# Two-part float32r products: one 512-column matmul over both parts of the activations, the halves added behind

## The chip, the cores and the metric

One core of one Trainium2 chip runs the kernel. The metric is device time in microseconds (us) of one execution. TensorE (PE) multiplies, with weight loads (PEld) beside its products; VectorE (DVE), ScalarE (ACT) and GpSimd (POOL) do the elementwise work; SyncE (SP) issues most of the DMAs.

## What is computed

Two transformer blocks of different make, one after the other, on 256 tokens of 1024 features, all in float32. The first has two layers: sparse attention with an output projection, a feed-forward, dilated attention with an output projection, a feed-forward. The second has one layer: a feed-forward, a mixer of three branches (indexed attention, a state-space layer, attention to a memory) with an output projection, a feed-forward. There are thus four feed-forwards of 2816 hidden features:

```python
def swiglu(h, w_up, w_down):
    a, b = jnp.split(h @ w_up, 2, axis=-1)
    return (jax.nn.silu(a) * b) @ w_down

x = x + swiglu(rmsnorm(x, norm_ffn[layer]), ffn_w_up[layer], ffn_w_down[layer])   # first block
x = x + 0.5 * swiglu_ffn(rms_norm(x, ffn1_norm[l]), ffn1_w_in[l], ffn1_w_out[l])  # second block
```

and three output projections of 1024x1024 (`... @ w_out`) that are added to x.

## The kernel before

Activations are held transposed: a tile is 128 features (partitions) by 256 tokens (S = 256). x is eight such tiles.

Precision: a float32 operand is split into two parts of type float32r, a high part (a rounding copy, on ACT) and a low part (the difference, on DVE). A product of two split operands is the sum of three products: high weight with high activations (line 228), high weight with low activations (229), low weight with high activations (230). `mm3` issues them for every weight block of 128x128 into one PSUM bank; the weight block is the stationary operand, the 256 columns of an activation part are the moving one. So each weight block costs three matmuls of 256 columns, and each of them loads its stationary operand. The page writes a matmul as out<-moving,stationary: `ov<-hh,wh` is high part of hidden block by high weight.

Weights come from HBM in loads of 128 x 8 x 256 float32 (1 MB, line 178, on SP's queue; tile `raw`, four buffers). `split` (lines 187 and 188) makes `wh` on ACT and `wl` on DVE, 1024 columns at a time (8 blocks, one projection's worth of the up phase), with four buffers of each.

`proj` takes the next PSUM bank (in the wide stages a rotation over seven of the eight banks, `take`) and runs `mm3` over all blocks of the inner dimension.

`ffn`, up phase: for each of 22 hidden blocks two projections (gate and up) over 8 blocks of x. DVE multiplies each with the row factors R of the norm while it reads PSUM (lines 393 and 395), ACT applies Silu (396), DVE multiplies (397), ACT and DVE split the hidden block into `hh` and `hl` (400, 401), which are two tiles. Down phase, `out_proj`: for each of 8 output tiles one projection over 22 hidden blocks, then one DVE multiply-add into x (411). The three output projections of attention and mixer go through `out_proj` too, with 8 blocks each. `gsplit` and `split_act` make the two parts of x and of attention outputs, as two tiles.

The order of instructions on each engine is made by a planner which lists them by priority and a modelled timeline; a stage's loads and splits so run ahead of it, and side work (the preparation of the state-space layer, `s5_prepare`, and the norm of the memory, `mem_norm`) lies where the planner found room: between 540 and 660 us, in the up phase of the second feed-forward. Buffers and semaphores follow from that order; every engine works its own list in order.

## Time and profile before

| | |
|---|---|
| median of 3 runs | 1362.96 us (1362.46 to 1367.53) |
| the profiled execution | 1365.27 us, its span 1363.5 us |
| TensorE busy | 1336.2 us (98%), 10944 products |
| weight loads busy | 1266.6 us (93%) |
| DVE busy | 1003.5 us (74%) |
| ACT busy | 746.7 us (55%) |
| POOL busy | 185.2 us (14%) |
| granted clock of TensorE | 0.994 |
| DMA | 232.77 MB, mean 171 GB/s |

The page gives busy time by engine, the span in 40 slices, the chain that ended last, and the costliest groups of instructions. A row of a group reads: line, engine, operation, tiles as out<-in, shape and type, count, then busy time in us, mean time of one in ns, idle time of the engine ahead of them with what ended it. Matmuls are pipelined, and each is printed with a length that overlaps the next: the cost of one in a stream is the distance of the starts.

### The profile page before, as it was taken

The numbers are of one execution on the slowest core, as the hardware profiler recorded it, in microseconds if no ns is written. First come the engines' busy times: TensorE is split into PE (matmuls) and PEld (weight loads), VectorE is DVE, ScalarE is ACT, GpSimd is POOL, SyncE is SP. The second block draws the span as 40 slices with busy tenths as digits, with TensorE's granted clock in tenths as the row PEclk, the third lists the DMA queues.
The fourth block names the chain that finished last, engine by engine and source line by source line (L and its number), as shares of the span: only waits on it lengthen the run. The fifth ranks groups of instructions, "written<-read, shape, count | busy, mean of one in ns | idle before, by whom it ended". The sixth has DMA issues, their size and how long they took to land.

```text
span 1363.5 us, 27489 instructions
## 1 busy us (share of the span) xinstructions
PE 1336.2 (98%) x10944; PEld 1266.6 (93%) x10944; DVE 1003.5 (74%) x2119; ACT 746.7 (55%) x1414; POOL 185.2 (14%) x225
## 2 busy tenths in 40 slices
PE   8999999999999999999999999999999999999997
PEld 7886999999998887999999999999987879999997
DVE  6899677766797663998955877755598897777643
ACT  4677555545668785754544555544433565544442
POOL 4200100001210000322100310001121044000011
PEclk9999999999999999999999999999999999999999
DMA  9741365545766350466856465556744254555451
GB/s 287 245 157 63 109 200 187 186 140 195 238 212 181 104 140 9 153 199 201 259 178 208 156 212 191 179 171 203 222 132 147 78 170 155 190 187 188 152 194 50
DMA packets 227120, 232.77 MB, mean 171 GB/s; under 512 B 5944, under 2 KB 221184, under 8 KB 226992
## 3 DMA queue, kind: packets, MB, share of 16 engines
q1 hardware_dynamic: 223392, 226.14, 52.3%
q10 hardware_dynamic: 3600, 4.88, 1.0%
q8 instruction: 86, 1.41, 0.4%
q14 instruction: 42, 0.34, 0.1%
HBM read 226.69 MB, written 4.30 MB: 169 GB/s over the span
## 4 chain that ended last, share of the span: by engine, by line
PE 85%; DVE 8%; DMA 2%; issue 2%; ACT 1%; POOL 1%; SPq 0%; POOLq 0%; DVEq 0%; ACTq 0%
PE mm L228 10%; PE mm L230 10%; PE mm L229 10%; PE tr L230 6%; PE tr L228 6%; PE tr L229 6%; PE sc L230 6%; PE sc L228 6%; PE sc L229 5%; PE ov L473 3%; PE ov L228 3%; PE ov L230 3%; PE ov L229 3%; DVE wl L188 3%; PE sc L777 2%
## 5 line engine op out<-in xcount | busy, mean ns | idle before, releaser
L187 ACT ACTIVATE wh<-raw 128x1024 fp32r<-128x1024 f32 (+2 forms) x405 | 417.8, 1036 | 449.9 <-PE mm L229 158.9
L188 DVE TENSOR_TENSOR wl<-raw,wh 128x1024 fp32r<-128x1024 f32 (+2 forms) x405 | 491.9, 1217 | 167.4 <-ACT wh L187 162.9
L228 PE MATMUL mm<-xh,wh 128*128 128x256 f32 x952 | 270.9, 285 | 2.4 <-ACT wh L187 2.4
L229 PE MATMUL mm<-xl,wh 128*128 128x256 f32 x952 | 270.9, 285 | 0.0
L230 PE MATMUL mm<-xh,wl 128*128 128x256 f32 x952 | 269.9, 284 | 0.5 <-DVE wl L188 0.5
L228 PEld LDWEIGHTS mm<-xh,wh 128*128 128x128 f32 x952 | 181.2, 190 | 9.7 <-issue 5.3
L230 PEld LDWEIGHTS mm<-xh,wl 128*128 128x128 f32 x952 | 180.7, 190 | 5.5 <-issue 4.0
L229 PEld LDWEIGHTS mm<-xl,wh 128*128 128x128 f32 x952 | 181.2, 190 | 3.1 <-issue 2.8
L293 POOL TENSOR_TENSOR sqacc<-sqacc,sq 128x256 f32<-128x256 f32 x60 | 61.8, 1033 | 602.7 <-ACT sq L292 326.1
L228 PE MATMUL sc<-xh,wh 128*128 128x256 f32 x464 | 129.7, 279 | 1.8 <-ACT wh L187 1.8
L230 PE MATMUL sc<-xh,wl 128*128 128x256 f32 x464 | 129.5, 279 | 0.2 <-DVE wl L188 0.2
L229 PE MATMUL sc<-xl,wh 128*128 128x256 f32 x464 | 129.5, 279 | 0.0
L230 PE MATMUL tr<-xh,wl 128*128 128x256 f32 x440 | 123.1, 280 | 0.4 <-DVE wl L188 0.4
L229 PE MATMUL tr<-xl,wh 128*128 128x256 f32 x440 | 122.8, 279 | 0.0
L228 PE MATMUL tr<-xh,wh 128*128 128x256 f32 x440 | 122.8, 279 | 0.0
L228 PEld LDWEIGHTS sc<-xh,wh 128*128 128x128 f32 x464 | 87.6, 189 | 2.0 <-ACT wh L187 2.0
L229 PEld LDWEIGHTS sc<-xl,wh 128*128 128x128 f32 x464 | 87.6, 189 | 0.0
L230 PEld LDWEIGHTS sc<-xh,wl 128*128 128x128 f32 x464 | 87.2, 188 | 0.4 <-DVE wl L188 0.4
L230 PEld LDWEIGHTS tr<-xh,wl 128*128 128x128 f32 x440 | 82.7, 188 | 0.6 <-DVE wl L188 0.6
L229 PEld LDWEIGHTS tr<-xl,wh 128*128 128x128 f32 x440 | 83.1, 189 | 0.0
L228 PEld LDWEIGHTS tr<-xh,wh 128*128 128x128 f32 x440 | 83.1, 189 | 0.0
L228 PE MATMUL ov<-xh,wh 128*128 128x256 f32 x224 | 62.7, 280 | 0.0
(481 smaller groups left out, 3404.9 us busy)
## 6 DMA issues: line engine op xcount, KB each, us to landing
raw<-in_ffn_w_up_dram SPq DMA_DIRECT2D x44, 1024.0 KB, 5.3
raw<-in_ffn_w_in_dram SPq DMA_DIRECT2D x44, 1024.0 KB, 5.3
raw<-in_w_in_dram SPq DMA_DIRECT2D x17, 1024.0 KB, 5.4
raw<-in_ffn_w_down_dram SPq DMA_DIRECT2D x16, 1024.0 KB, 5.2
raw<-in_ffn_w_out_dram SPq DMA_DIRECT2D x16, 1024.0 KB, 5.2
raw<-in_b_w_q_dram SPq DMA_DIRECT2D x12, 1024.0 KB, 5.2
raw<-in_a_w_in_dram SPq DMA_DIRECT2D x8, 1024.0 KB, 8.7
bt<-u_scratch SPq DMA_DIRECT2D x28, 256.0 KB, 4.5
```

Of the source, the lines that this page charges most:

```text
L187: nc.scalar.activation(hv, v, AF.Copy)
L188: nc.vector.tensor_tensor(lv, v, hv.bitcast(F32), ALU.subtract)
L228: nc.tensor.matmul(ps, sh, mh, start=(i == 0), stop=False)
L229: nc.tensor.matmul(ps, sh, ml, start=False, stop=False)
L230: nc.tensor.matmul(ps, sl, mh, start=False, stop=(i == n - 1))
L293: nc.gpsimd.tensor_tensor(acc[:, 0], acc[:, 0], s, ALU.add)
L473: nc.tensor.matmul(O[64 * i:64 * i + 64, q0:q1], V[kb], pt[:, c0:c0 + q1 - q0], start=(start and kb == 0), stop=(stop and kb == 1), skip_g ...
L777: nc.tensor.matmul(ps, Q[d, h][:, qb * P:qb * P + P], K[d][g], start=(i == 0), stop=(i == 1))
```

## The change

`mm2` takes the place of `mm3` in the feed-forwards and in `out_proj`. The two parts of an activation block now lie side by side in one tile of 512 columns (`parts`): the high weight meets both in one product of 512 columns that fills a whole PSUM bank, and the low weight meets the high part in one product of 256 columns that adds to the bank's first half. The result is the sum of the bank's halves. In the up phase `joined` makes it: ACT copies the second half to SBUF (`fc`), DVE adds the first half to it, POOL multiplies with R, which DVE did before. In `out_proj` DVE adds each half to x in a multiply-add of its own. The buffers of `fa` and `fb` go from two to three, `fc` has three. Other projections keep `mm3`, on the halves of the joint tiles.

```diff
--- before.py
+++ after.py
@@ -224,10 +224,18 @@
 
         nc = self.nc
         n = len(pairs)
-        for i, ((sh, sl), (mh, ml)) in enumerate(pairs):
+        for i, ((sh, sl), (mh, ml, *_)) in enumerate(pairs):
             nc.tensor.matmul(ps, sh, mh, start=(i == 0), stop=False)
             nc.tensor.matmul(ps, sh, ml, start=False, stop=False)
             nc.tensor.matmul(ps, sl, mh, start=False, stop=(i == n - 1))
+
+    def mm2(self, ps, pairs):
+
+        nc = self.nc
+        n = len(pairs)
+        for i, ((sh, sl), (mh, _, mhl)) in enumerate(pairs):
+            nc.tensor.matmul(ps, sh, mhl, start=(i == 0), stop=(i == n - 1), skip_group_check=True)
+            nc.tensor.matmul(ps[:, :S], sl, mh, start=False, stop=(i == n - 1), skip_group_check=True)
 
     def bank(self, tag):
         return getattr(self, tag).tile([P, 512], F32, tag=tag, name=self.n(tag))
@@ -246,23 +254,33 @@
         self.mm3(o, list(zip(unit, X)))
         return o
 
+    def proj2(self, unit, X):
+
+        o = self.take()
+        self.mm2(o, list(zip(unit, X)))
+        return o[:, :S], o[:, S:]
+
     def proj_tok(self, wide, X, tb, cols):
         o = self.take()[:, :cols]
         sl = slice(tb * P, tb * P + P)
-        self.mm3(o, [((xh[:, sl], xl[:, sl]), w) for (xh, xl), w in zip(X, wide)])
+        self.mm3(o, [((xh[:, sl], xl[:, sl]), w) for (xh, xl, _), w in zip(X, wide)])
         return o
+
+    def parts(self, pool, tag, name, **kw):
+
+        hl = pool.tile([P, 2 * S], F32R, tag=tag, name=self.n(name), **kw)
+        return hl[:, :S], hl[:, S:], hl
 
     def split_act(self, src, name, k, pool=None, flip=False):
 
         nc = self.nc
         src = flipped(src) if flip else blocks(src)
         pool, pre = (pool, name) if pool else (self.xs_pool, "x")
-        h = pool.tile([P, S], F32R, tag=f"{pre}h{k}", name=self.n(name + "h"))
-        l = pool.tile([P, S], F32R, tag=f"{pre}l{k}", name=self.n(name + "l"))
+        h, l, hl = self.parts(pool, f"{pre}{k}", name)
         h3, l3 = blocks(h), blocks(l)
         nc.scalar.activation(h3, src, AF.Copy)
         nc.vector.tensor_tensor(l3, src, h3.bitcast(F32), ALU.subtract)
-        return h, l
+        return h, l, hl
 
 
     def gain(self, name, k):
@@ -271,11 +289,10 @@
     def gsplit(self, x, g, k):
 
         nc = self.nc
-        h = self.xs_pool.tile([P, S], F32R, tag=f"xh{k}", name=self.n("xh"))
-        l = self.xs_pool.tile([P, S], F32R, tag=f"xl{k}", name=self.n("xl"))
+        h, l, hl = self.parts(self.xs_pool, f"x{k}", "x")
         nc.scalar.activation(h, x, AF.Copy, scale=g)
         nc.vector.scalar_tensor_tensor(l, x, g, h.bitcast(F32), ALU.mult, ALU.subtract)
-        return h, l
+        return h, l, hl
 
     def sq_begin(self):
         return self.tmp.tile([P, 2, S], F32, tag="sqacc", name=self.n("sqacc"), bufs=1)
@@ -387,28 +404,33 @@
                 ub = self.units(w_up, D, FF + mp * 256)
                 for c in range(2):
                     k = 2 * mp + c
-                    pa = self.proj(next(ua), X)
-                    pb = self.proj(next(ub), X)
-                    a = hp.tile([P, S], F32, tag="fa", name=self.n("fa"), bufs=2)
-                    nc.vector.tensor_tensor(a, pa, R, ALU.mult)
-                    b = hp.tile([P, S], F32, tag="fb", name=self.n("fb"), bufs=2)
-                    nc.vector.tensor_tensor(b, pb, R, ALU.mult)
+                    a, b = (self.joined(hp, next(u), X, R, t) for u, t in ((ua, "fa"), (ub, "fb")))
                     nc.scalar.activation(a, a, AF.Silu)
                     nc.vector.tensor_tensor(b, a, b, ALU.mult)
-                    h = hp.tile([P, S], F32R, name=self.n("hh"), tag=f"hh{k}")
-                    l = hp.tile([P, S], F32R, name=self.n("hl"), tag=f"hl{k}")
+                    h, l, hl = self.parts(hp, f"h{k}", "hh")
                     nc.scalar.activation(h, b, AF.Copy)
                     nc.vector.tensor_tensor(l, b, h.bitcast(F32), ALU.subtract)
-                    H.append((h, l))
+                    H.append((h, l, hl))
             self.out_proj(xs, w_down, FF, H, factor)
+
+    def joined(self, pool, unit, X, R, tag):
+
+        nc = self.nc
+        p, q = self.proj2(unit, X)
+        t = pool.tile([P, S], F32, tag="fc", name=self.n("fc"), bufs=3)
+        nc.scalar.activation(t, q, AF.Copy)
+        a = pool.tile([P, S], F32, tag=tag, name=self.n(tag), bufs=3)
+        nc.vector.tensor_tensor(a, p, t, ALU.add)
+        nc.gpsimd.tensor_tensor(a, a, R, ALU.mult)
+        return a
 
     def out_proj(self, xs, w, K, X, factor):
         nc = self.nc
         for mp in range(4):
             for c, u in enumerate(self.units(w, K, mp * 256)):
-                ps = self.proj(u, X)
                 m = 2 * mp + c
-                nc.vector.scalar_tensor_tensor(xs[m], ps, float(factor), xs[m], ALU.mult, ALU.add)
+                for ps in self.proj2(u, X):
+                    nc.vector.scalar_tensor_tensor(xs[m], ps, float(factor), xs[m], ALU.mult, ALU.add)
 
 
     def bias_rows(self):
```

## Rows read from the trace of the kernel before

**Rows 1.** The page: its head and the first line of section 1.

```profile
span 1363.5 us, 27489 instructions
PE 1336.2 (98%) x10944; PEld 1266.6 (93%) x10944; DVE 1003.5 (74%) x2119; ACT 746.7 (55%) x1414; POOL 185.2 (14%) x225
```

**Rows 2.** Table of stretches: start:end, length, busy us (count) by engine, clock, DMA.

```profile
171.00:350.00 179.00, 179.00 (x1522) 179.00 (x1522) 124.27 (x176) 91.85 (x131) 6.03 (x6) 1.00 0.58 186
560.00:680.00 120.00, 118.92 (x1037) 118.12 (x1036) 114.01 (x312) 68.28 (x108) 29.65 (x44) 1.00 0.65 208
685.00:745.00 60.00, 60.00 (x514) 60.00 (x513) 30.31 (x34) 25.74 (x31) 4.36 (x3) 1.00 0.60 196
797.00:880.00 83.00, 83.00 (x735) 83.00 (x734) 62.29 (x96) 43.78 (x64) 0.00 (x0) 1.00 0.60 192
888.00:945.00 57.00, 57.00 (x484) 57.00 (x483) 34.14 (x39) 26.88 (x37) 5.83 (x6) 1.00 0.59 188
1173.00:1288.00 115.00, 115.00 (x979) 115.00 (x978) 83.90 (x127) 58.87 (x84) 0.00 (x0) 1.00 0.56 182
1290.00:1349.00 59.00, 59.00 (x494) 59.00 (x493) 28.04 (x31) 23.43 (x29) 7.79 (x6) 1.00 0.40 130
```

**Rows 3.** Longest wait of TensorE from 560 to 680: us in total, times, longest.

```profile
PE tr L230 <- DVE wl L188: 0.4, 1, 0.4
```

**Rows 4.** Timeline of TensorE, second feed-forward up: start, length, instruction.

```profile
620.04 0.28 PE L228 MATMUL sc<-xh,wh 128*128 128x256 f32 x1
...
629.89 0.28 PE L228 MATMUL mm<-xh,wh 128*128 128x256 f32 x1
```

**Rows 5.** Timeline of TensorE: products of 512 columns in the first attention.

```profile
85.15 0.40 PE L642 MATMUL sc<-KH,q 128*128 128x512 f32 x1
85.39 0.39 PE L642 MATMUL sc<-KL,q 128*128 128x512 f32 x1
85.62 0.28 PE L230 MATMUL mm<-xh,wl 128*128 128x256 f32 x1
...
89.39 0.39 PE L642 MATMUL sc<-KH,q 128*128 128x512 f32 x1
89.61 0.39 PE L642 MATMUL sc<-KL,q 128*128 128x512 f32 x1
89.84 0.28 PE L229 MATMUL mm<-xl,wh 128*128 128x256 f32 x1
```

**Rows 6.** Groups by shape: the split from 171 to 265, the others over the span.

```profile
L188 DVE TENSOR_TENSOR wl<-raw,wh 128x1024 fp32r<-128x1024 f32 x34 | 41.7, 1226 | 10.5 <-ACT wh L187 9.4
L395 DVE TENSOR_TENSOR fb<-sc,R 128x256 f32<-128x256 f32 x26 | 10.9, 421 | 10.1 <-PE sc L230 10.1
L411 DVE SCALAR_TENSOR_TENSOR x<-tr,x 128x256 f32<-128x256 f32 x17 | 7.2, 421 | 13.4 <-PE tr L230 13.3
L810 ACT ACTIVATE Rd<-tr 128x256 f32<-128x256 f32 x8 | 3.0, 376 | 3.8 <-PE tr L808 3.7
```

**Rows 7.** Groups by shape over the span: POOL, and DVE beside it.

```profile
L1017 POOL TENSOR_TENSOR vr<-vr,t 128x256 f32<-128x256 f32 x8 | 5.9, 741 | 40.9 <-DVE t L1014 40.9
L490 POOL TENSOR_TENSOR KL<-kt,KH 64x256 fp32r<-64x256 f32 x20 | 20.1, 1005 | 22.4 <-ACT KH L487 21.5
L488 DVE TENSOR_TENSOR KL<-kt,KH 64x256 fp32r<-64x256 f32 x20 | 16.9, 845 | 0.3
L502 DVE TENSOR_TENSOR q<-qt,q 64x256 fp32r<-64x256 f32 x64 | 26.9, 420 | 2.0
```

**Rows 8.** Group of DVE from 560 to 680: the weight split.

```profile
L188 DVE TENSOR_TENSOR wl<-raw,wh 128x1024 fp32r<-128x1024 f32 x43 | 54.4, 1266 | 0.6 <-ACT wh L187 0.6
```

**Rows 9.** Timeline at the end of the last feed-forward.

```profile
1354.13 0.42 DVE L411 SCALAR_TENSOR_TENSOR x<-tr,x 128x256 f32<-128x256 f32 x1 [7.71 <-PE tr L230]
```

**Rows 10.** Timeline of TensorE where the first feed-forward ends.

```profile
350.28 0.28 PE L230 MATMUL tr<-hh,wl 128*128 128x256 f32 x1
350.40 0.28 PE L228 MATMUL mm<-xh,wh 128*128 128x256 f32 x1
```

## The prediction

> **What bounds the kernel now.** I read the page's busy shares first, then a table of stretches cut by stage, then the waits, then single products in the timeline. The busy shares name TensorE: 1336.2 of 1363.5 us [rows 1]. A share of busy time is an average, so the question is what each stage that the change touches waits for. Seven stretches lie inside the four feed-forwards [rows 2]: 171 to 350 is the whole first one, then come up and down of the second, the third and the fourth. In six of them TensorE is busy in every microsecond at a granted clock of 1.00 (2.4 GHz), DVE for 47 to 75% and ACT for 40 to 53%. DMA moves 130 to 196 GB/s with its engines busy for 0.40 to 0.60. These stages are worth what their products cost, one after the other. The seventh stretch, the up phase of the second feed-forward (560 to 680), differs: DVE is busy for 114.0 of 120 us there, its weight splits wait 0.6 us in all for their input [rows 8], and the longest wait of TensorE is for such a split [rows 3]. There DVE stands right behind TensorE.
>
> The price of a product is start to start, not the printed duration (products overlap). By stretch, busy time over products, less two that lap over the edges [rows 2]: first feed-forward 179/1520 = 0.1178 us; down phases of the other three 0.1172, 0.1183 and 0.1199; up of the third 0.1132; up of the fourth 0.1177. Up of the second, without its waits: 87 products from 620.04 to 629.89, 0.1132 [rows 4]. So 256 columns cost 0.113 to 0.120 where 256 cycles of 2.4 GHz are 0.1067: each product carries 0.0065 to 0.0133 on top, and the up phases at 0.1132 and at 0.1177 run the same code.
>
> **The change, part by part.** Products. Per weight block there were three of 256 columns; now there are one of 512 and one of 256. Blocks: a feed-forward has 44 x 8 going up and 8 x 22 coming down, 528, times four, 2112; the three output projections of attention and mixer have 64 each, 192; together 2304. TensorE spends on them now: first feed-forward 1584 x 0.1178 = 186.6; second 1056 x 0.1132 + 528 x 0.1172 = 181.4; third 119.5 + 62.5 = 182.0; fourth 124.3 + 63.3 = 187.6; the 576 products of the output projections at about 0.115 (an estimate between the two levels) 66.2. Sum 803.8 us.
>
> What does a product of 512 columns cost? The kernel has a few of the same operand type, in the scores of the first attention: start to start 0.22, 0.23, 0.24, 0.23 [rows 5], a mean of 0.23 with the last figure rounded. Those stand singly among other work. From the long streams: the common 256-column step of 0.1178 less 0.1067 is 0.0111 on top per product; with the same on top, 512 columns are 0.2133 + 0.0111 = 0.2244, the lower end of those rows. I take 0.2244, because an unbroken stream is what the feed-forwards are, and 0.1175 for the other product: 0.3419 per block, 2304 x 0.3419 = 787.7, a gain of 16.1 us. It is all of one kind: one of three amounts on top is dropped. Best end: 0.2133 + 0.0065 for the wide one and 0.1132 for the narrow one, 0.333, gain 36.6. Worst end: 0.24 and 0.1199, 0.360, loss 25; the 0.24 came once, so 0.23 + 0.1199 = 0.350, a loss of 2.5, is the end that I carry. The two stretches at 0.1132 gain nothing at my price (0.3396 now); the gain comes from the first and the fourth feed-forward and the down phases.
>
> The Trainium skill, "TensorE: Matmul & The Clock Gate", section "Back-to-back issue gap", speaks against the change: it gives a warm product its columns over 2.4 GHz plus 2.5 ns, and by that dropping a product would save 2304 x 0.0025 = 5.8 us. The trace doesn't agree with 2.5 ns here, since the least step of the streams has 6.5 ns on top.
>
> Halves, up phase. For each of 176 products (44 in each feed-forward) DVE's multiplication by R, 0.42 [rows 6], becomes an addition of the same size and operands (PSUM and SBUF): nothing. ACT gets a copy of 128x256 out of PSUM, 0.376 by a like copy [rows 6]: 44 x 0.376 = 16.5 us per up phase of some 120 us, on an engine that is half idle [rows 2]; covered. POOL gets the multiplication by R, 0.74 undisturbed [rows 7]: 44 x 0.74 = 32.6 us per up phase, on an engine that is idle in the first, third and fourth. In the chain to the hidden block, copy, POOL and three hand-overs add 1.3 us or more; the last hidden block is wanted only behind the first 21 blocks of the down product (21 x 0.342 = 7.2 us), so I cost it at nothing; without that cover it is some 2 us for each feed-forward. PSUM banks rotate over seven products of 2.7 us; one more reader does not fill them.
>
> What POOL does to DVE is the dearest unknown. Where both subtract the same tile in two halves, DVE's 64x256 takes 0.845 in place of 0.420, and POOL 1.005 [rows 7]: 0.425 per POOL instruction when DVE follows at once. The weight split, with two inputs from SBUF too, takes 1.226 in the quiet up phase and 1.266 in the second, where POOL works for 29.7 us [rows 2, 6, 8]. So a POOL instruction costs DVE between nothing and its own 0.74; I take 0.25, since a good third of DVE's work (the additions, and its idle time) takes nothing from POOL. In three up phases that is 11 us on an engine with 30 us to spare: covered by the splits made ahead. In the second, 44 x 0.25 = 11 us meets 6 us of idle time: TensorE waits 5 us more.
>
> The Trainium skill, "SBUF — State Buffer", section "Who interferes with whom", has this as a rule: a DVE instruction with two inputs from SBUF contends with a POOL instruction that reads SBUF, and whoever comes second waits for the whole of the other. The trace agrees for DVE's 0.845. By the rule's full wait, 0.74 each, the second up phase would lose 32.6 - 6 = 27 us; that is the third case below.
>
> Halves, down phase. Each of 56 output tiles gets a second multiply-add of 0.42 [rows 6]: 3.4 us per stage, beside an idle DVE. Between stages the first projection of the next stage follows without a gap (350.28 to 350.40 [rows 10]); I put 1 us for the six joints (0 to 2.5). At the very end it is bare: the last multiply-add begins when TensorE is done [rows 9], so +0.4.
>
> One tile for both parts: the first product waits for high and low part together, where it waited for the high one. That falls into the same 1 us. Loads, splits and queues of DMA stay as they are; 2 MB per 10.9 us in place of 11.3 asks 4% more of DMA engines that have a third of their time free.
>
> Sum: 16.1 - 5 - 1 - 0.4 = 9.7 us. The profiled execution took 1365.27 us (span 1363.5, 1.8 around it), 0.2% over the median of 1362.96. From it: 1355.6; set against the median: **1353 us**.
>
> **The rivals.** (1) The wide product has the price of the mean row, 0.23: 0.3475 per block, 800.6, a gain of 3.2, which the 6.4 us of other terms eat: 1366 us. For it: the rows themselves. Against it: in the streams the step is constant for tens of microseconds. (2) POOL holds DVE for its whole 0.74 in the second up phase: 1353 + 22 = 1375 us, slower. It decides from the point where the price reaches 0.62 per POOL instruction (then 27 - 6 = 21 us of waits use up what is left of the gain and the half per cent). For it: DVE has 6 us left in that stretch. Against it: 0.425 is the highest that the rows show. (3) The streams settle in the cheap step, 0.333 per block: 1353 - 20 = 1333 us. For it: two up phases run at 0.1132 now, with the same code. (4) Instructions are ordered by a planner, and new durations give a new order in every stage: some 4 us either way, 1357 us if it goes against the kernel. That the products are not saved is not among the rivals; 2304 fewer are in the code.
>
> **How the numbers follow.** Forecast 0.48, (1) 0.21, (2) 0.14, (3) 0.08, (4) 0.09. A measurement tells about 0.5% (6.8 us) from no change, so faster means below 1356.1 and slower above 1369.8. Faster: (3) and nine tenths of the forecast, with a little of (4), 0.53; slower: (2) and a little of (1), 0.16; the rest, 0.31, is no change. The range runs from 1337 (half of (3) left out) to 1372 (most of (2) left out).
>
> **What would show it.** TensorE's products 2304 fewer; in the stretch of the first feed-forward a pair of steps of 0.224 and 0.118 where three of 0.118 stood; the first feed-forward shorter by some 6 us and the fourth by 7, the up phases of the second and third not shorter. A longer second up phase with DVE at its limit, and waits of TensorE for the weight split, would be case (2); the weight split's mean there tells the price. A wide step of 0.23 is case (1). The forecast is wrong if the narrow product behind a wide one costs other than 0.113 to 0.120, or if products wait for hidden blocks at the start of a down phase.

## The result, and the profile after

The changed kernel is slower: 1384.15 us (median of four runs, 1382.57 to 1385.62) against 1363.22 us for the kernel before in the same comparison. The ratio is 1.0154, with a 95% interval of 1.0138 to 1.0170. The forecast was 1353 us with a range up to 1372; it was wrong in sign and range. The profiled execution took 1385.62 us, its span 1383.8 us, 20.3 us more than before [rows 1].

First line of section 1 of the page after (engine, busy us, share, instructions), the answer to [rows 1]:

```profile
PE 1349.8 (98%) x8640; PEld 1168.6 (84%) x8640; DVE 1040.0 (75%) x2175; ACT 790.9 (57%) x1590; POOL 343.3 (25%) x401
```

The 2304 products are gone (10944 to 8640), and TensorE is still busy for 13.6 us longer. The table of stretches after (start:end, length, busy us and count of PE, PEld, DVE, ACT, POOL, clock, DMA share, GB/s), the same seven stages as [rows 2]:

```profile
180.00:350.00 170.00, 170.00 (x965) 147.69 (x964) 120.96 (x178) 98.19 (x169) 42.46 (x50) 1.00 0.58 187
575.00:700.00 125.00, 117.80 (x643) 100.00 (x642) 121.07 (x277) 70.88 (x132) 64.97 (x81) 0.97 0.55 175
708.00:766.00 58.00, 58.00 (x336) 51.06 (x336) 34.79 (x44) 27.45 (x35) 6.14 (x6) 1.00 0.63 205
815.00:900.00 85.00, 85.00 (x485) 73.92 (x484) 62.76 (x96) 51.54 (x94) 26.65 (x31) 1.00 0.58 184
912.00:968.00 56.00, 56.00 (x319) 48.61 (x319) 36.52 (x45) 27.29 (x37) 6.47 (x7) 1.00 0.62 193
1195.00:1305.00 110.00, 110.00 (x627) 95.68 (x627) 80.17 (x122) 68.19 (x123) 35.27 (x41) 1.00 0.57 181
1314.00:1372.00 58.00, 58.00 (x337) 50.71 (x336) 29.84 (x38) 22.52 (x28) 8.26 (x7) 1.00 0.41 132
```

A block is now two products, so its price is length over half the count (less two at the edges): 0.353 in the first feed-forward, 0.352 in the third and fourth up phase, 0.353 in the third down phase, 0.347 and 0.346 in the second and fourth down phase. The forecast had 0.342 everywhere. Only the second stretch has TensorE idle, 7.2 us of 125, and only there the granted clock is below 1.00. Single pairs, from the timeline (start, printed length, instruction):

```profile
249.60 0.40 PE L237 MATMUL mm<-x,wh 128*128 128x512 f32 x1
249.84 0.28 PE L238 MATMUL mm<-x,wl 128*128 128x256 f32 x1
249.96 0.40 PE L237 MATMUL mm<-x,wh 128*128 128x512 f32 x1
...
257.38 0.40 PE L237 MATMUL ov<-x,wh 128*128 128x512 f32 x1
```

From the first to the last are 22 pairs in 7.78 us, 0.3536 each: the wide product (line 237) takes 0.235, the narrow one (238) 0.118. The forecast had 0.2244 and 0.1175.

In the second up phase, 572 to 700 us, TensorE's longest waits (us in total, times, longest):

```profile
PE ov L238 <- DVE wl L188: 1.5, 2, 1.3
PE ov L316 <- POOL sqacc L310: 1.5, 1, 1.5
PE sc L237 <- ACT wh L187: 1.3, 1, 1.3
```

and groups of DVE and POOL in the same stretch (busy us, mean ns, idle time and its cause):

```profile
L188 DVE TENSOR_TENSOR wl<-raw,wh 128x1024 fp32r<-128x1024 f32 x39 | 49.4, 1266 | 0.7 <-ACT wh L187 0.6
L409 DVE TENSOR_TENSOR fb<-fa,fb 128x256 f32<-128x256 f32 x19 | 10.1, 533 | 2.1 <-POOL fb L424 2.1
...
L424 POOL TENSOR_TENSOR fa<-fa,R 128x256 f32<-128x256 f32 x20 | 19.4, 972 | 24.4 <-DVE fa L423 17.6 <-DVE sl L1009 4.4 <-DVE CS L1001 1.5
```

TensorE waits for weight splits and for POOL, over a microsecond at a time, where its longest wait was 0.4 us before, from 560 to 680 us [rows 3]. The weight split has 0.7 us of idle time left, as before [rows 8]. DVE's product of the two hidden halves (L409), with both inputs in SBUF, takes 0.53 in the mean, and 0.418 in the same stretch of the trace before; POOL's multiplication is printed with 0.97 where 0.74 was taken from [rows 7].

How the wait of 1.3 us for ACT comes about stands in ACT's timeline and in TensorE's behind it:

```profile
589.52 0.42 ACT L408 ACTIVATE fa<-fa 128x256 f32<-128x256 f32 x1 [0.85 <-POOL fa L424]
591.40 0.42 ACT L411 ACTIVATE hh<-fb 128x256 fp32r<-128x256 f32 x1 [1.47 <-DVE fb L409]
...
592.44 1.04 ACT L187 ACTIVATE wh<-raw 128x1024 fp32r<-128x1024 f32 x1
...
593.53 0.51 PE L237 MATMUL sc<-x,wh 128*128 128x512 f32 x1 [1.32 <-ACT wh L187]
```

ACT's Silu waits for POOL's multiplication, its split of the hidden block for DVE's product, and the weight split stands behind both in ACT's list. TensorE got only a few products between 591.8 and 596.0 us, and its clock fell:

```profile
594.70:601.52 6.82, 5.98 (x21) 5.30 (x22) 6.78 (x18) 3.48 (x7) 3.30 (x5) 0.50 0.23 68
```

At 0.50 (1.2 GHz) a pair took 0.64 us, 0.353 at 1.00. The 5.98 us of busy time would have been about 3.0 at the full clock, so up to 3.0 us of what this stage lost are the clock's (an estimate). The same happened in the sparse attention, from 133.90 to 137.31 us (3.41 us busy at 0.50, up to 1.7 us); the kernel before has such a fall at 764.40 us instead, as long, in its third feed-forward.

Where the 20.3 us went, by stage. A stage is counted here from one output or down projection's last multiply-add into x to the next one's, read from the traces (us), one execution for each column. The kernels of the later columns are the experiments below. The last row is the median over all executions of a kernel; those of "out only" spread from 1364.1 to 1374.6 us, and the one traced took 1365.4.

| stage | before | after | joint tiles | out only | up only | feed-forward only | no R | R on DVE | place |
|---|---|---|---|---|---|---|---|---|---|
| sparse attention | 165.7 | 173.0 | 164.1 | 170.5 | 164.1 | 163.5 | 171.5 | 170.0 | 171.9 |
| feed-forward 1 | 185.4 | 183.5 | 185.4 | 179.2 | 185.3 | 186.2 | 183.5 | 183.5 | 179.9 |
| dilated attention | 213.2 | 215.2 | 213.3 | 215.2 | 213.0 | 212.6 | 215.1 | 215.3 | 216.8 |
| feed-forward 2 | 184.5 | 196.6 | 185.8 | 186.9 | 196.9 | 195.8 | 186.7 | 186.8 | 195.3 |
| feed-forward 3 | 202.2 | 204.2 | 200.5 | 200.3 | 204.6 | 204.3 | 203.7 | 203.7 | 201.6 |
| mixer | 215.5 | 218.3 | 215.0 | 218.0 | 214.8 | 214.8 | 218.1 | 218.2 | 220.0 |
| feed-forward 4 | 188.2 | 183.5 | 187.5 | 184.4 | 187.8 | 186.7 | 183.5 | 183.5 | 181.0 |
| end | 8.9 | 9.4 | 8.9 | 8.9 | 9.0 | 8.9 | 9.0 | 9.4 | 9.5 |
| median time | 1363.2 | 1384.2 | 1362.4 | 1369.4 | 1379.2 | 1374.6 | 1371.9 | 1372.3 | 1378.5 |

The second feed-forward (+12.1) and the sparse attention (+7.3) carry most of it; no feed-forward gains what the forecast gave it.

### The profile page after: what moved, and what is told of

It is laid out like the page before. It is cut to its first block, busy times and chain, and to the rows that moved or that the text cites. A ratio compares the mean times of both kernels' runs of the same rounds, so it can differ in the third digit from the quotient of the medians.

```text
span 1383.8 us, 23364 instructions
## 1 busy us (share of the span) xinstructions
PE 1349.8 (98%) x8640; PEld 1168.6 (84%) x8640; DVE 1040.0 (75%) x2175; ACT 790.9 (57%) x1590; POOL 343.3 (25%) x401
## 4 chain that ended last, share of the span: by engine, by line
PE 82%; DVE 11%; issue 3%; ACT 1%; POOL 1%; DMA 1%; SPq 0%; DVEq 0%; POOLq 0%; ACTq 0%
PE mm L237 10%; PE tr L237 9%; PE sc L237 9%; PE mm L228 5%; PE mm L230 5%; PE mm L229 5%; PE mm L238 5%; PE ov L237 5%; PE tr L238 5%; PE sc L238 5%; PE ov L495 3%; DVE wl L188 3%; PE ov L238 2%; PE sc L799 2%; PE ov L1051 1%
## 5 line engine op out<-in xcount | busy, mean ns | idle before, releaser
L187 ACT ACTIVATE wh<-raw 128x1024 fp32r<-128x1024 f32 (+2 forms) x405 | 417.4, 1035 | 399.1 <-PE tr L237 79.6
L228 PE MATMUL mm<-x,wh 128*128 128x256 f32 x552 | 159.0, 288 | 2.2 <-ACT wh L187 2.2
L230 PE MATMUL mm<-x,wl 128*128 128x256 f32 x552 | 157.9, 286 | 1.7 <-DVE wl L188 1.7
L229 PE MATMUL mm<-x,wh 128*128 128x256 f32 x552 | 158.5, 287 | 0.0
L237 PE MATMUL mm<-x,wh 128*128 128x512 f32 x400 | 146.6, 402 | 0.0
L237 PE MATMUL sc<-x,wh 128*128 128x512 f32 x400 | 144.6, 397 | 1.3 <-ACT wh L187 1.3
L237 PE MATMUL tr<-x,wh 128*128 128x512 f32 x400 | 144.6, 398 | 0.3 <-DVE x L294 0.3
L424 POOL TENSOR_TENSOR fa<-fa,R 128x256 f32<-128x256 f32 x88 | 83.3, 946 | 161.8 <-DVE fa L423 146.1
L238 PE MATMUL mm<-x,wl 128*128 128x256 f32 x400 | 114.1, 285 | 0.6 <-DVE wl L188 0.4
L238 PE MATMUL sc<-x,wl 128*128 128x256 f32 x400 | 112.9, 282 | 1.3 <-DVE wl L188 1.3
L228 PEld LDWEIGHTS mm<-x,wh 128*128 128x128 f32 x552 | 105.4, 191 | 9.5 <-issue 5.3
L238 PE MATMUL tr<-x,wl 128*128 128x256 f32 x400 | 112.7, 282 | 0.3 <-DVE wl L188 0.3
L230 PEld LDWEIGHTS mm<-x,wl 128*128 128x128 f32 x552 | 105.0, 190 | 6.7 <-issue 4.0
L229 PEld LDWEIGHTS mm<-x,wh 128*128 128x128 f32 x552 | 105.2, 191 | 3.0 <-issue 2.8
L237 PEld LDWEIGHTS mm<-x,wh 128*128 128x128 f32 x400 | 76.1, 191 | 18.0
L238 PEld LDWEIGHTS mm<-x,wl 128*128 128x128 f32 x400 | 76.2, 191 | 1.9 <-DVE wl L188 1.4
```

The costliest lines, as they stand in the source:

```text
L187: nc.scalar.activation(hv, v, AF.Copy)
L228: nc.tensor.matmul(ps, sh, mh, start=(i == 0), stop=False)
L229: nc.tensor.matmul(ps, sh, ml, start=False, stop=False)
L230: nc.tensor.matmul(ps, sl, mh, start=False, stop=(i == n - 1))
L237: nc.tensor.matmul(ps, sh, mhl, start=(i == 0), stop=(i == n - 1), skip_group_check=True)
L238: nc.tensor.matmul(ps[:, :S], sl, mh, start=False, stop=(i == n - 1), skip_group_check=True)
```

## The experiments

### Which part of the change loses

Each kernel was run beside the kernel before; the ratio given is to that, with its 95% interval. Four kernels take the change apart. The first keeps three products and the evacuations of before in joint tiles; the second has the pair in output and down projections alone, the third in the up phases alone, the fourth in the feed-forwards (up and down) but not in the three output projections of attention and mixer.

```diff
 # up phase as before ("joint tiles" and "out only")
-                    a, b = (self.joined(hp, next(u), X, R, t) for u, t in ((ua, "fa"), (ub, "fb")))
+                    pa = self.proj(next(ua), X)
+                    ...
 # out_proj as before ("joint tiles" and "up only"); "feed-forward only":
-                for ps in self.proj2(u, X):
+                for ps in (self.proj2(u, X) if K == FF else [self.proj(u, X)]):
```

> The change without its products: both parts of an activation in one tile of 512 columns, but three products of 256 columns per block and the evacuations of before, in feed-forwards and output projections alike. If the loss comes from joint tiles and the new order that the planner makes of them: 1371 to 1378 us, with the first attention some 7 us longer as after the change. If it comes from the products and their evacuation: 1360 to 1366 us, all stages as before.

Measured: 1362.41 us, ratio 0.9991 [0.9982, 1.0001]. The joint tile costs nothing, as the forecast had it: its share of "1 us for the joints" may go.

> The pair of 512 and 256 columns in the output and down projections alone; the up phases keep three products and one multiplication by R on DVE out of PSUM, with no copy on ACT and nothing on POOL. 'Per product' (896 blocks save 0.011 each): 1363 - 10 = 1353 us. 'With the columns' and stage by stage as the changed kernel: attentions and mixer keep their losses (7.3 + 2.0 + 2.8 us), the second feed-forward loses its 12 us no more: 1370 to 1377 us. If the attentions' loss comes from elsewhere: 1360 to 1366 us.

Measured: 1369.39 us, ratio 1.0045 [1.0012, 1.0077], just under the range given for "with the columns". The attentions and the mixer keep their losses; the second feed-forward is nearly back. The first feed-forward is 6.2 us shorter than before, and not by its down phase: its up phase, whose code is that of the joint tiles, ran at another step. The same stretch with joint tiles:

```profile
180.00:260.00 80.00, 80.00 (x682) 80.00 (x681) 57.65 (x86) 40.37 (x58) 0.00 (x0) 1.00 0.57 187
```

and with "out only":

```profile
180.00:260.00 80.00, 80.00 (x708) 80.00 (x708) 60.95 (x93) 42.98 (x63) 0.00 (x0) 1.00 0.64 208
```

80/680 = 0.1176 and 80/706 = 0.1133 for the same products out of the same addresses. That is the difference which the prediction saw between up phases and left unexplained; more on it below.

> The pair of 512 and 256 columns in the up phases alone (with the copy on ACT, the addition on DVE and the multiplication by R on POOL); output and down projections keep three products and one multiply-add. 'Per product' (1408 blocks save 0.011 each, less 5 us in the second up phase): 1363 - 10 = 1353 us. 'With the columns': second feed-forward 12 us longer, the rest within some us: 1370 to 1378 us; if the attentions' loss comes from the output projections, the first attention is back at 166 us.

Measured: 1379.22 us, ratio 1.0109 [1.0090, 1.0127]. The second feed-forward loses its 12 us here, and the attentions nothing. Against the joint tiles, "out only" adds 7.0 us and "up only" 16.8; with the -2.3 of the tiles themselves that makes 21.5, and the whole change lost 20.9. The two parts add up, as far as the spread of "out only" lets one say.

> The change in the four feed-forwards (up and down), while the three output projections of attention and mixer keep three products of 256 columns and one multiply-add. If the losses of the attentions and the mixer (7.3 + 2.0 + 2.8 us) come from the pair in their output projections: 1384 - 12 = 1372 us, the first attention at 164 to 166 us. If they come from the joint tiles or the order: 1380 to 1386 us.

Measured: 1374.56 us, ratio 1.0077 [1.0054, 1.0100]: 9.6 us less than with the pair everywhere. The three stages are at 163.5, 212.6 and 214.8 us, no longer than before. So the pair in the output projections of attention and mixer costs 10 us, which the forecast had inside "1 us for the six joints".

How they do it shows at the end of the sparse attention. The weight splits of the next blocks (ACT, L187) start when earlier blocks give their buffers back: in the timeline of ACT with joint tiles

```profile
147.89 2.96 ACT L187 ACTIVATE wh<-raw 128x1024 fp32r<-128x1024 f32 x3 [3.03 <-PE tr L229]
```

with "out only"

```profile
150.66 3.91 ACT L187 ACTIVATE wh<-raw 128x1024 fp32r<-128x1024 f32 x4 [3.38 <-PE tr L237]
```

and in the timeline of TensorE of "out only" behind it:

```profile
152.72 0.50 PE L237 MATMUL mm<-o,wh 128*128 128x512 f32 x1 [0.45 <-ACT wh L187]
153.67 0.49 PE L237 MATMUL sc<-o,wh 128*128 128x512 f32 x1 [0.44 <-ACT wh L187]
```

With the pair the first buffer comes free 2.8 us later, ACT then makes four splits in a row at about 1 us each, and TensorE issues one product for each split where it would issue many. From 140 to 172 us the starts of "out only" that are over 0.26 us apart hold 2.7 us over the price of their products (0.235 wide, 0.115 narrow), those of the joint tiles 0.6. With 64 blocks at 0.353 in place of 0.340 (0.9 us) this accounts for about half of the 6.4 us between the two; where the rest lies is not shown. The changed kernel has the fall of the clock on top, which "out only" hasn't: 173.0 and 170.5 us.

### What a wide product costs

> Computes nothing of the reference: isolated streams of float32r products without any other engine at work, each stream behind a short wait. Streams: three 256-column products per weight block (as before), one 512 and one 256 (as after), 512 alone, 256 alone, 256 with one stationary operand, 128 and 64 columns; the first two with the moving operand at eight places (32 bytes apart), three and two times each. Theory 'with the columns': what a product costs over its columns at 2.4 GHz grows with the columns, so a 512-column step is 2.0 times the 256-column step of the same place (0.227 by 0.1132, 0.236 by 0.118), a pair costs what three narrow ones cost (0.340 to 0.354), and a 128-column step is half a 256-column one (0.057 to 0.059). Rival 'per product' (the prediction's premise): 512 columns take 0.2133 + 0.0111 = 0.224, 128 columns 0.0533 + 0.0111 = 0.064, and the pair is about 0.011 cheaper than three. Theory 'place': the step is 0.113 or 0.118 by the moving operand's place, the same in each repeat of a place. Rival 'state': the step differs between repeats of one place, since what happens at the wait sets it.

The kernel ran 60 streams, each of one kind; price of a block in us, from start to start over 13 blocks of each stream, repeats side by side. The place is moving less stationary address modulo 256 bytes, from the kernel's memory layout.

| place | three of 256 columns | 512 and 256 |
|---|---|---|
| 0 | 0.3596, 0.3596, 0.3595 | 0.3530, 0.3464 |
| 32 | 0.3502, 0.3501, 0.3503 | 0.3467, 0.3470 |
| 64 | 0.3533, 0.3533, 0.3400 | 0.3487, 0.3535 |
| 96 | 0.3602, 0.3603, 0.3602 | 0.3505, 0.3499 |
| 128 | 0.3563, 0.3600, 0.3559 | 0.3507, 0.3508 |
| 160 | 0.3559, 0.3558, 0.3518 | 0.3468, 0.3466 |
| 192 | 0.3400, 0.3400, 0.3400 | 0.3533, 0.3529 |
| 224 | 0.3551, 0.3552, 0.3552 | 0.3539, 0.3526 |

Two rows of a stream of three and two of a stream of pairs, both at place 192:

```profile
53.14 0.28 PE L150 MATMUL ps<-mv,st 128*128 128x256 f32 x1
...
57.90 0.28 PE L150 MATMUL ps<-mv,st 128*128 128x256 f32 x1
...
206.98 0.40 PE L156 MATMUL ps<-mv,st 128*128 128x512 f32 x1
...
211.93 0.40 PE L156 MATMUL ps<-mv,st 128*128 128x512 f32 x1
```

Each lies 14 blocks apart: 4.76/14 = 0.340 for three, 4.95/14 = 0.3536 for the pair. x and the weights of both kernels stand at place 192. There the pair is never cheaper than three narrow products: it costs what three cost at their common step (0.3534), and three have a cheaper one (0.340). Over all places the least pair is 0.3464, above the least three. Alone, 512 columns took 0.2294 and 0.2324 by place, 256 columns 0.1198 and 0.1200. So what a product costs over its columns is not one amount per product: 0.0131 on 256 columns, 0.016 to 0.019 on 512 in these rows, and 0.022 on the wide one of the pair at place 192. Neither theory holds at every place. At 0, 96, 128 and 160 the pair is cheaper than three, by 0.005 to 0.013, about as "per product" has it; at 32 and 224 by 0.001 to 0.004; at 192, where it counts here, it costs as much as three at the upper step, as "with the columns" has it, and 0.013 more than three at the lower. The place sets most of the price; at places 0, 64, 128 and 160 repeats differ, so it isn't all of it.

Changing stationary places with the moving one at a fixed place gave the same prices at the same difference (192: 0.3400 twice; 32: 0.3500 twice).

Does it carry over? The next kernel puts x and hidden blocks of the changed kernel at place 160 by other pads.

```diff
-        self.pad(e(tc.tile_pool(name="pad0", bufs=1)), 192)
+        self.pad(e(tc.tile_pool(name="pad0", bufs=1)), 160)
-        self.pad(e(tc.tile_pool(name="pad1", bufs=1)), 320)
+        self.pad(e(tc.tile_pool(name="pad1", bufs=1)), 352)
 # skew of the four feed-forwards: 0, 320, 320, 416 -> 224, 320, 256, 320
```

> The changed kernel with x and all hidden blocks 160 bytes above the weights modulo 256 (only the sizes of the pads differ), where the isolated pair took 0.347 in place of 0.3534 at 192. If that carries over: 1760 of the 2112 blocks (all but the second down phase, which lies there already) save 0.0065 each, 11 us: 1370 to 1375 us, still above the kernel before. If the place only counts without the other engines: 1380 to 1386 us.

Measured: 1378.54 us, ratio 1.0102 [1.0083, 1.0120]. The first feed-forward, table of stretches:

```profile
180.00:345.00 165.00, 165.00 (x954) 145.24 (x953) 118.58 (x175) 96.82 (x168) 41.01 (x48) 1.00 0.59 191
```

165/476 = 0.3466 per block, the price of the isolated streams. The time is above the 1370 to 1375 us expected of that. The four feed-forwards are 10 us shorter together (767.8 to 757.8); the attentions and the mixer, whose three-product projections left place 192, gave 2 us back, and 1378.5 is 6 us under the changed kernel. The products of the change are now as cheap as the streams ever showed them, and the kernel is still slower than before.

### What POOL costs

> Computes nothing of the reference. First part: isolated streams of three 256-column products per block, the moving operand 192 bytes above the stationary one modulo 256, where the streams before all ran at 0.1135, now each entered in another way: from a wait, behind one to five products of 128 columns, behind pairs of 512 and 256, directly behind a stream at another place. If the place alone sets the step: 0.113 to 0.114 in each. If the step is a state that is kept from the entry on: 0.1178 behind some of them, as in the first and fourth feed-forward before. Second part: DVE's weight split of 128x1024 out of SBUF, its 128x256 with two inputs from SBUF, and its 128x256 with one from PSUM, each alone and beside a row of POOL multiplications of 128x256. If POOL costs DVE about what the prediction took: 0.25 us of DVE time for each POOL instruction; if DVE waits for the whole of POOL: 0.74; if nothing: the same means in both.

The first part answers little: its streams ran while the second part worked, and several of them at a granted clock of 0.50, where 256 columns took 0.2133, exactly their columns at 1.2 GHz. The next study repeats it. The second part, by groups (busy us, mean ns): DVE's weight split alone and beside POOL, POOL beside it, DVE's 128x256 out of SBUF alone and beside POOL, out of PSUM alone and beside POOL:

```profile
L189 DVE TENSOR_TENSOR big<-src,raw 128x1024 fp32r<-128x1024 f32 x8 | 9.3, 1222 | 3.3 <-ACT src L185 3.3
...
L189 DVE TENSOR_TENSOR big<-src,raw 128x1024 fp32r<-128x1024 f32 x8 | 12.9, 1681 | 1.1 <-ACT src L185 1.1
L201 POOL TENSOR_TENSOR dst<-src,raw 128x256 f32<-128x256 f32 x8 | 13.4, 1705 | 0.5 <-ACT src L185 0.5
...
L193 DVE TENSOR_TENSOR big<-src,raw 128x256 fp32r<-128x256 f32 x16 | 5.5, 424 | 3.7 <-ACT src L185 3.7
...
L193 DVE TENSOR_TENSOR big<-src,raw 128x256 fp32r<-128x256 f32 x13 | 10.9, 906 | 0.4 <-ACT src L185 0.4
...
L197 DVE TENSOR_TENSOR big<-acc,src 128x256 fp32r<-128x256 f32 x8 | 2.7, 414 | 0.0
...
L197 DVE TENSOR_TENSOR big<-acc,src 128x256 fp32r<-128x256 f32 x16 | 5.5, 415 | 0.4 <-ACT src L185 0.4
```

The means beside POOL hold one or two instructions that met no POOL. Those that did lasted 1.74 to 1.755 in place of 1.22 in most cases, and 0.94 to 0.955 in place of 0.42: 0.53 us for each POOL instruction, whatever the length of DVE's own. An input from PSUM pays nothing (0.414 and 0.415). POOL pays as well: 1.705 beside the split, 0.73 alone. The prediction took 0.25 and called 0.425 the highest that the rows show [rows 7]. The trace before did show the price: three of the 43 splits of its second up phase took 1.77, 1.76 and 2.06, each beside a POOL instruction. The first of them and an undisturbed one:

```profile
574.88 1.77 DVE L188 TENSOR_TENSOR wl<-raw,wh 128x1024 fp32r<-128x1024 f32 x1
...
578.84 1.21 DVE L188 TENSOR_TENSOR wl<-raw,wh 128x1024 fp32r<-128x1024 f32 x1
```

The mean of all, 1.266 [rows 8], hid it.

The Trainium skill, "SBUF — State Buffer", section "Who interferes with whom", names this pair, a DVE instruction with two SBUF inputs and a POOL instruction that reads SBUF. The runs agree on which instructions pay; on the size, a wait for the whole of the other would be 0.73, and 0.53 was measured.

> The changed kernel without POOL's multiplications by R in the feed-forwards (this part of the computation is left out, so the norm's row factor is missing). If POOL's hold on DVE is what stretches the second up phase: its waits fall from some 13 to 3 us, and the total from 1384 to 1374 to 1378 us. If the waits there come from the order, the copies on ACT or the step of the products: 1381 to 1386 us.

```diff
-        nc.gpsimd.tensor_tensor(a, a, R, ALU.mult)
         return a
```

Measured: 1371.88 us, ratio 1.0057 [1.0042, 1.0072]: 12.3 us less than with them, a little more than the most that was expected. The second feed-forward returns 9.9 of them (196.6 to 186.7). Its clock did not fall in the second up phase, so up to 3.0 of these are the clock's (an estimate, as above).

> The changed kernel with the multiplication by R on DVE, behind the addition, in place of POOL: 44 more DVE instructions of 128x256 out of SBUF in each up phase, at 0.42 us alone 18.5 us, and no POOL beside them. If POOL's price of 0.53 us (a POOL multiplication beside a DVE instruction with two inputs from SBUF) fell on nearly every multiplication, DVE gains 44 x 0.11 = 5 us in the second up phase: 1379 us. If it fell on half of them or fewer, DVE loses 7 us or more there: 1391 us or more. If the waits came from POOL's place in the chain of the hidden block and not from DVE: about 1375 us.

```diff
-        nc.gpsimd.tensor_tensor(a, a, R, ALU.mult)
+        nc.vector.tensor_tensor(a, a, R, ALU.mult)
         return a
```

Measured: 1372.25 us, ratio 1.0056 [1.0039, 1.0072], lower than each theory had it and equal to leaving R out; the nearest is the third, POOL's place in the chain (1375). Second up phase, tables of stretches, after the change (R on POOL):

```profile
572.00:700.00 128.00, 120.80 (x662) 102.68 (x661) 122.90 (x290) 73.65 (x138) 64.97 (x81) 0.97 0.56 178
```

without R:

```profile
572.00:700.00 128.00, 125.98 (x719) 109.19 (x718) 115.13 (x296) 80.06 (x149) 33.59 (x42) 1.00 0.59 193
```

with R on DVE:

```profile
572.00:700.00 128.00, 126.73 (x716) 110.22 (x715) 124.41 (x336) 79.94 (x147) 27.98 (x42) 0.99 0.56 183
```

With R on DVE, DVE is busy for 124.4 of 128 us, more than after the change, and TensorE loses nothing by it. In that time it makes 45 weight splits where the changed kernel makes 39, and 44 multiplications on top. Printed lengths overlap a little; from start to start a split takes 1.17 there and a multiplication by R 0.36: 6 x 1.17 + 44 x 0.36 = 23 us more work in 1.5 us more of busy time. Spread over the 39 multiplications that POOL makes in this stretch, that is about 0.55 us of DVE for each (an estimate; the side work in the stretch differs a little), which agrees with 0.53. Doing it on DVE costs 0.36 by the same count. How much of the 12 us is this price, how much the chain (ACT's Silu waits for POOL, DVE's L409 waits 2.1 us for POOL's `fb`, and side work of POOL stands behind the multiplications) and how much the clock that falls behind such waits is not separated by these runs.

### What sets the step of three narrow products

> Computes nothing of the reference, and no other engine works beside the streams. Three 256-column products per block with the moving operand 192 bytes above the stationary one modulo 256, each stream entered without a wait from 24 products at another place: from 64 (where the streams before went on at 0.1178) or from 0 (where they went on at 0.1133). In the middle of the stream stands a kick: one to four products of 128 columns, one or two of 64, one to three of 256 at place 0, or three at place 0 in the order of a block. If the step is a state that the order of products passes on: every stream entered from 64 runs at 0.1178 and every one from 0 at 0.1133, twice alike, and some kicks change 0.1178 into 0.1133 (two of 128 columns did so once). If it is chance: the two repeats differ.

A kick is a product or a few of another kind in the middle of a stream. Behind 24 products at place 0 all 22 streams at place 192 went on at 0.1133. Behind 24 at place 64, which ran at 0.1177 to 0.1179 themselves, sixteen went on at 0.1178 and six at 0.1133, and the two repeats differed for six of the eleven. So the entry isn't wholly set by the order of products; but each stream kept its level up to the kick, and the kicks show a rule. Level behind a kick, by the level ahead of it (number of streams):

| kick | from 0.1178 | from 0.1133 |
|---|---|---|
| one of 128 columns | 0.1178 (1) | 0.1178 (3) |
| two or three of 128 | 0.1133 (4) | 0.1133 (4) |
| four of 128 | 0.1178 (1) | 0.1133 (3) |
| one of 64 | 0.1133 (2) | 0.1178 (2) |
| two of 64 | 0.1133 (2) | 0.1133 (2) |
| one of 256 at place 0 | 0.1178 (1) | 0.1133 (3) |
| two of 256 at place 0 | 0.1133 (2) | 0.1178 (2) |
| three of 256 at place 0 | 0.1133 (2) | 0.1133 (6) |

In the last line stand also the three in a block's order. The same kick from the same level gave the same result each time. Two products of 128 columns end in the cheap level from either. A level that is passed on is the right theory there, with an entry that these runs do not explain.

Two kernels try this on the kernel before: one with all hidden blocks at place 192 (they stood at 192, 160, 224 and 0 there), and the same with kicks.

```diff
 # skew of the second, third and fourth feed-forward: 320, 320, 416 -> 352, 288, 352
 # with kicks also:
-        self.mm3(o, list(zip(unit, X)))
+        pairs = list(zip(unit, X))
+        for _ in range(2 * kick):
+            self.nc.tensor.matmul(o[:, :P], pairs[0][0][0], pairs[0][1][0][:, :P], start=True, stop=True)
+        self.mm3(o, pairs)
 # kick is k in (1, 8, 15) for the gate projection, and m == 1 in the down phases
```

> The kernel before with the hidden blocks of all four feed-forwards 192 bytes above the weights modulo 256 (only the sizes of the pads differ), where three narrow products took 0.340 alone. If the place sets the step: the down phases of the second, third and fourth run at 0.1135 in place of 0.1172, 0.1183 and 0.1199, 528 x (0.0037 + 0.0048 + 0.0064) = 8 us less: 1355 us. If the step is a state that is kept from the entry: 0.1178 in the fourth, and 1358 to 1364 us.

Measured: 1357.62 us, ratio 0.9953 [0.9938, 0.9968]. The third feed-forward ran at 0.1133 from end to end (202.2 to 197.8 us), the first, second and fourth at 0.1178: the second up phase, at 0.1132 before, fell into the dear level. Place alone does not decide.

> The kernel before with all hidden blocks 192 bytes above the weights (as in the run with the pads changed) and, at four points of each feed-forward, two products of 128 columns ahead of a projection (into its bank, which the projection then overwrites). If the step of 0.1178 is a state that such a kick turns into 0.1133 in the full kernel too: the first, second and fourth feed-forward (1584 products each) save 0.0045 each, 21 us, less 16 kicks of 0.23 us, 3.7: 1357.6 - 17.7 = 1340 us. If the work of the other engines sets the step: 0.1178 stays in these stages, 1358 to 1362 us.

Measured: 1351.02 us, ratio 0.9906 [0.9885, 0.9928]: it beats both kernels. A stretch of the first feed-forward with the pads alone:

```profile
215.00:340.00 125.00, 125.00 (x1064) 125.00 (x1063) 84.92 (x116) 63.04 (x90) 5.03 (x5) 1.00 0.55 180
```

with the kicks:

```profile
215.00:340.00 125.00, 125.00 (x1105) 125.00 (x1104) 87.93 (x122) 65.76 (x94) 5.05 (x5) 1.00 0.58 187
```

and the timeline around the second kick, at 209.33:

```profile
208.86 0.28 PE L230 MATMUL sc<-xh,wl 128*128 128x256 f32 x1
...
209.21 0.28 PE L230 MATMUL sc<-xh,wl 128*128 128x256 f32 x1
209.33 0.33 PE L248 MATMUL tr<-xh,wh 128*128 128x128 f32 x2
209.50 0.33 PE L228 MATMUL tr<-xh,wh 128*128 128x256 f32 x1
...
210.13 0.28 PE L230 MATMUL tr<-xh,wl 128*128 128x256 f32 x1
...
210.47 0.28 PE L230 MATMUL tr<-xh,wl 128*128 128x256 f32 x1
```

Three products take 0.35 ahead of the kick and 0.34 behind it, and 125/1062 = 0.1177 becomes 125/1103 = 0.1133 for the whole stretch. The gain over the pads alone is 6.6 us where 17.7 were expected: the first kick of a feed-forward stands ahead of four or eight products of 128 columns that belong to the norm (L317), and behind those the step was 0.1178 in all four up phases; the first and the fourth keep it up to the second kick, a third of the way. The one at 169.1 us was undone by

```profile
170.84 0.60 PE L317 MATMUL ov<-con,rr 128*128 128x128 f32 x4
```

The later kicks were all followed by 0.1133 and kept it, but for the third of the second up phase (645.4 us): behind a wait of 0.4 us for a weight split, at 649.3, the step was 0.1178 up to the next kick at 693.7.

The trace before reads the same way. The norm's products (L314 there) end at 170.9, 570.4, 771.1 and 1173.2 us, and behind each the step is 0.1178. The first and the fourth up phase have no other products between and keep it to their end; in the second and the third side work of 128 columns or less follows, and behind the last of it the step is 0.1133 or close to it. The line of the norm and the last of side work in the third:

```profile
770.26 1.05 PE L314 MATMUL ov<-con,rr 128*128 128x128 f32 x8
...
796.32 0.38 PE L1103 MATMUL tr<-con,hb 128*128 128x128 f32 x2
```

So two up phases of the same code differ by what stands between their products. It isn't a rule that tells the level ahead: with "out only" the norm's products of the first up phase were followed by 0.1133.

## Why the prediction was wrong, point by point

**The price of the wide product (the step that failed first).** "With the same on top, 512 columns are 0.2133 + 0.0111" assumed that a product's surplus is one amount. No row of before showed that; the rows of 512 columns [rows 5] had 0.22 to 0.24 and were overruled by it. The trace after has 0.235 beside 0.118. Per block 0.3533 (place 192) or 0.3467 (160, 0) in place of 0.3419: by these prices the feed-forwards cost 186.5 + 185.4 + 186.5 + 185.4 and the output projections 192 x 0.3533 = 67.8, together 811.6 us where the same sum had 803.8 before. The term is a loss of 7.8, not a gain of 16.1. Rival (1) came nearest, with 0.3475; the worst end that was carried, 0.350, was too low by 0.003, and the dropped one (0.24 and 0.1199) too high.

**The up phases at 0.1132.** "Gain nothing" was wrong by 4.8 us each: 352 x (0.3533 - 0.3396). They had the cheap level of three narrow products, and no pair has it at this place. The prediction saw two levels under the same code and took them for a property of the stage; they are levels of the stream, which other products and waits between change.

**POOL beside DVE.** The mechanism and its place were right: the second up phase lost, with DVE at its limit and TensorE waiting for weight splits. The term was 5 us; leaving POOL's multiplications out returns 12.3. The price was taken as 0.25 and is 0.53 by itself, about 0.55 in the stage (the estimate above); single splits of the trace before had it, 1.77 in place of 1.22. Rival (2) put its deciding point at 0.62, and its full 0.74 was not reached. "A good third of DVE's work takes nothing" was right as to kind (PSUM inputs pay nothing) and of no help, because the work that pays is what TensorE waits for. The sum also overlooked that POOL itself slows down, 0.73 to 0.97 and more, with side work and ACT's Silu behind it, and that the clock can fall behind such waits (up to 3.0 us, an estimate).

**Output projections of attention and mixer.** Costed as products and 1 us of joints. They cost 9.6 us, up to 1.7 of them the clock's. That the order of a planner can go against the kernel was rival (4), at 4 us and a chance of 0.09; it was too small, and the place was wrong: not every stage, but the three with an output projection. How is shown for about half of the first alone (buffers that come free later); the rest stays open.

**The end and the joint tile.** The second multiply-add at the end was put at 0.4 us; 8.9 became 9.4. The joint tile by itself costs nothing. ACT's copies were costed at nothing, and no wait here is shown to be theirs: the 1.3 us in the second up phase are for a weight split on ACT that stood behind Silu and the hidden block's split, which waited for POOL and DVE. With "three hand-overs" at nothing, the chain was left out of the sum there.

**The sum by stages.** Products in the feed-forwards +6.2, the rest of the second feed-forward +8.1 (up to 3.0 of them the clock's), attentions and mixer +12.1, the end +0.5, and the first, third and fourth feed-forward 6.8 us shorter than their products make them: 20.1 of the 20.3 us. The last item is not explained by a run of its own. The fall of the clock in the third feed-forward before (up to 1.7 us), which the changed kernel hasn't, is part of it; and with the pair in feed-forwards alone the first and the fourth are longer by 2.7 and 3.2, so it is in part what a late output projection hands on to the next stage.

## What to carry to other kernels

Don't split a price into "work plus an amount per instruction" unless rows at two sizes show it in the same stream; where the trace has the larger instruction itself, its row goes ahead of the model. Look at single instructions, not only at a group's mean: three splits of 43 held the price of POOL. Before an elementwise step moves to POOL, ask what DVE does then: each POOL instruction on SBUF took 0.53 us from a DVE instruction with two SBUF inputs, more than DVE's own 0.42 for the step. Where a stage starts to wait, look at its granted clock too. And when the same code runs at two steady speeds in one trace, find out why before summing with either: a kernel made from that difference is 0.9% faster than the one before, 12 us, more than the 9.7 that the change was to give.

## What the runs showed of the hardware

The step of a 256-column float32r product lay between 0.1133 and 0.1201 us by the difference of moving and stationary address modulo 256, and at one difference it could have two values (0.1133 and 0.1178 at 192), kept over a thousand products. Two products of 128 columns between them set it to the lower one in each of the isolated trials and, in the kernel, until a wait or the norm's products of 128 columns raised it again. At a granted clock of 0.50 the surplus was gone (0.2133).

Products of 128 columns, each with its weights, were no cheaper than 0.1117, so neither theory's figure (0.058 or 0.064) held; row of the table of stretches for that stream:

```profile
342.00:348.00 6.00, 6.00 (x56) 6.00 (x56) 0.00 (x0) 0.00 (x0) 0.00 (x0) 1.00 0.00 0
```

A stream of 64 columns had the same step at the full clock, 0.1117, and 0.2133 at a granted clock of 0.50. What both have in common is a weight load of 128 columns for each product, so the step goes with the load and not with the product's columns. The Trainium skill, "TensorE: Matmul & The Clock Gate", section "LDWEIGHTS (loading the stationary operand)", gives a load its columns over 1.2 GHz. That is 0.1067 for 128 (an estimate by its formula), close to the 0.1117 here. The Trainium skill, "TensorE: Matmul & The Clock Gate", section "Back-to-back issue gap", cited in the prediction with 2.5 ns, is contradicted by all streams of 256 and 512 columns here at the full clock (6.7 to 22 ns on top).
